# Encoder layer on one core: z multiplied in as the heads' outputs leave PSUM, two buffers in turn for the short convolutions, and operand splits one step ahead

## Chip, cores and metric

The kernel runs on one core of one Trainium2 chip. The metric is the device time of one execution in microseconds (us); lower is better. Times before were taken in three runs, and one more execution was recorded by the hardware profiler.

## The reference, cut to what matters

One layer of a bidirectional encoder over 16 learned tokens and 1024 tokens, with a width of 1024, in float32:

```
h = RMSNorm(x); proj = h @ w_in
q, k, v, z, beta, a, sc_b, sc_c, sc_x, gate_a, gate_b = split(proj)
# branch A, 8 heads of 128: gated delta rule over chunks of 64, forward and backward
o   = o_fwd + o_bwd
o   = o * rsqrt(mean(o * o) + eps) * norm_w
o   = o * silu(z)
y_a = o @ w_branch_dn
# branch B: centred short convolution of width 3
y_b = (sc_b * dwconv3(sc_c * sc_x)) @ w_branch_sc
merged = sigmoid(gate_a) * y_a + sigmoid(gate_b) * y_b
x = x + merged @ w_out
x = x + SwiGLU(RMSNorm(x));  out = RMSNorm(x)
```

## The kernel before

Matmul operands in float32 are split in two parts, high and low, and a product is made of three matmuls (high by high, high by low, low by high). The engines' operations go through a small recorder, so the trace puts nearly all of them down to its line 189; the text goes by names of tiles instead.

**Phase 1 (0 to about 912 us)** has its order written out while the program is built. A model of the engines (class `Clock`) holds a time for each engine, and `run_streams` (line 1186) lets one of several generators go on whenever the modelled TensorE time has reached the time that it asked for. TensorE's filler is the projection `h @ w_in`, 128 columns at a time (`dense_steps`, tile `pm`). Between its matmuls run the steps of the eight heads: `g_decay`, `g_norm`, `g_meta`, `g_inv` (the inverse of a triangular matrix of 64 by 64, with tiles `W`, `XT`, `NP` and `T`), `g_vals`, `g_scan` (the recurrence, with state `S`) and `g_out`. VectorE has lanes of jobs of its own: convolutions of q, k and v, short convolutions, and a substitution.

What comes out of a projection is one of these. `u_z` (line 642) puts silu(z) of a head, in two halves of 128x512, through the buffer `rb` into the DRAM tensor `z_d`. `u_short` with `i` 0 or 1 builds the product of two projections, and then `short_job` (line 588) makes its convolution: for each half one scaling on ScalarE and two multiply-adds on VectorE, in the buffer `yb`, and a store to `yc_d`. `u_short` with `i` = 2 loads both halves again, into `rb` and `yb`, multiplies them with the third projection and stores them to `p_d`. `rb` (`half_buffer`, line 528) and `yb` (`conv_buffer`, line 531) are one buffer each.

`g_out` (line 1074) normalises a head's output, scales four chunks at a time by ScalarE, turns them by TensorE into a PSUM bank `pv`, takes that out by ScalarE with the norm's weight as the scale (`o<-pv,cols`) and stores it to `o_d`.

**The block products (about 915 to 1229 us).** Four stages, called `gb`, `ga` (the two gates), `sc` and `dn` (the two branches), each make a product of 1024x1024 by 1024x1024 out of seven products A to G of half the size (`seven`, line 1592). A product has four steps of 12 matmuls. Each step needs one quarter of its operand split, by ScalarE (`raw` or `wh`, high) and VectorE (`raw` or `wl`, low), into a ring of buffers (`halved`, line 1580). `between` lists work that is written in between the steps: loads of the next stage's blocks, their sums and differences (`by_two`, tiles `pair`), and in `gb` and `ga` also `times_z` (line 1692), which loads a head's `o_d` and `z_d`, multiplies them on VectorE (tiles `w` and `t`) and stores `o_d` again. `evict` takes finished banks out (tiles `s`). A scheduler with a model of its own puts these instructions in order on each engine.

After that come the projection by `w_out`, SwiGLU and the last norm, to the end of the span.

The lines in question of `short_job`, `seven` and `g_out` are among these:

Of the kernel before, what the change touches and what calls it, by code (L numbers as in the profile page):

```python
# [202 lines left out]
def encoder_layer(ctx: ExitStack, tc: tile.TileContext, x, meta, norm1_w, w_in,  # L203
# [323 lines left out]

    def half_buffer():
        return d1.tile([P, 512], F32, tag="rb", name=uid("rb"), bufs=1)

    def conv_buffer():
        return d1.tile([P, 512], F32, tag="yb", name=uid("yb"), bufs=1)

# [53 lines left out]

    def short_job(cx, j, ycs):
        for i in range(2):
            yc = conv_buffer()  # L590
            ycs.append(yc)
            nc.scalar.activation(yc[:, :512], cx[:, 1 + 512 * i:513 + 512 * i], AF.Copy, scale=cols[:, j:j + 1])
            yield A()
            for t in range(1, 3):
                nc.vector.scalar_tensor_tensor(out=yc[:, :512], in0=cx[:, 1 + t + 512 * i:1 + t + 512 * i + 512],
                                               scalar=cols[:, 8 * t + j:8 * t + j + 1], in1=yc[:, :512],
                                               op0=ALU.mult, op1=ALU.add)
                V()
                yield T["dve"] + DEP
            nc.sync.dma_start(yc_d[j][:, 512 * i:512 * i + 512], yc[:, :512])  # L600

    def u_short(j, i, w):
        st_ = shorts[j]
        if i < 2:
# [15 lines left out]
            if i == 1:  # L620
                run_late(True)
                st_["yc"] = []
                st_["job"] = enqueue("short", short_job(st_["cx"], j, st_["yc"]))
                raws[st_["ri"]] = st_["job"]
            else:
                st_["ri"] = len(raws) - 1
        else:
            force(shorts[-1]["job"])
            run_late(True)
            ycs = [half_buffer(), conv_buffer()]  # L630
            for i2 in range(2):
                nc.sync.dma_start(ycs[i2], yc_d[j][:, 512 * i2:512 * i2 + 512])
            for i2 in range(2):
                po = psm()
                yield from dense_steps(po, w, hx, META + 512 * i2, 512)

                def evict(yc=ycs[i2], po=po, i2=i2):
                    nc.vector.tensor_tensor(out=yc, in0=po, in1=yc, op=ALU.mult)
                    nc.sync.dma_start(p_d[j][:, 512 * i2:512 * i2 + 512], yc)
                later(pe(), evict)  # L640

    def u_z(h, w):

        for i in range(2):
# [3 lines left out]
            def evict(po=po, i=i):  # L648
                th = half_buffer()[:, :512]
                nc.scalar.activation(th, po, AF.Silu)  # L650
                nc.sync.dma_start(z_d[h][:, 512 * i:512 * i + 512], th)
            later(pe(), evict)

# [420 lines left out]
    def g_out(h, st_):  # L1074
# [14 lines left out]
        while not job.done:  # L1089
            yield T["pe"] + 300  # L1090
        yield after(y)
        for c4 in range(2):
            oT = O[:, 4 * c4:4 * c4 + 4]
            for c in range(4):
                nc.scalar.activation(oacc[4 * c4 + c], oacc[4 * c4 + c], AF.Copy, scale=y[:, 4 * c4 + c:4 * c4 + c + 1])
# [5 lines left out]
            for c in range(4):  # L1101
                transpose(pt[:, c], oacc[4 * c4 + c])
            yield pe()
            nc.scalar.activation(oT, pt, AF.Copy, scale=cols[:, 24:25])
            t = A()
            lock["scan"] = None
# [484 lines left out]

    def seven(pairs, X, Y, tok, evict, between, moving={}, snap=snap, last_first=False):

        p1s = u2s = p5s = None
        ready = []
        for n, (key, bank, first) in enumerate((("A", X, True), ("B", Y, True), ("C", X, False), ("D", Y, True),
# [3 lines left out]
            for k in range(4):  # L1600
                h_, l_ = ready.pop(0) if ready else halved(pairs[key], k, 512 if key in moving else D)
                bh, bl = moving[key](k) if key in moving else (h_[:, hi], l_[:, hi])
                for t in range(4):
                    c = slice(t * P, t * P + P)
                    for j, (a, b) in enumerate(((h_, bh), (h_, bl), (l_, bh))):
                        fresh = first and k == j == 0
                        mm(bank[t], a[:, c], b, start=fresh, stop=first and k == 3 and j == 2,
                           skip_group_check=not first)
                for f in between[n][1 + k]:
                    f()  # L1610
# [12 lines left out]
            else:  # L1623
                if last_first and n == 5:
                    ready = [halved(pairs["G"], k, D) for k in range(4)]
                evict(*((0, tok[0], bank, p1s), (1, tok[1], bank, p5s), (0, tok[1], bank, u2s))[(1, 4, 5).index(n)])
# [64 lines left out]

    def times_z(j):
        o_ = big("w2", [P, D], F32)
        nc.sync.dma_start(o_, o_d[j])
        for h_ in halves:
            z_ = tp.tile([P, 512], F32, tag="t2", name=uid("t2"), bufs=2)
            nc.sync.dma_start(z_, z_d[j][:, h_])
            nc.vector.tensor_tensor(out=o_[:, h_], in0=o_[:, h_], in1=z_, op=ALU.mult)
        nc.sync.dma_start(o_d[j], o_)

    during_gb = [
# [25 lines left out]
    for d, X, Y, dst, during in ((gb, bank_m, bank_d, tb_d, during_gb), (ga, bank_d, bank_m, ta_d, during_ga)):  # L1727
        seven(d, X, Y, (0, 1), evict_gate(dst), during, {"A": states(0, 0), "B": states(1, 0), "F": states(1, 1)},
              lambda n: pieces())

# [38 lines left out]
    def o_block(key, kh, half):  # L1769
# [17 lines left out]
        [[lambda: new(dn_, "D", "ah0")], [], [], [], []]]  # L1787
    seven(sc, bank_m, bank_d, (0, 1), evict_sc, during_sc)

# [388 lines left out]
```

## Time and profile before

| what | value |
|---|---|
| runs | 1958.40, 1960.96, 1962.62 us |
| median | 1960.96 us |
| profiled execution | 1964.22 us, its span 1962.50 us |
| granted clock of TensorE in it, mean | 0.998 |
| DMA, whole span | 275.76 MB, 141 GB/s |

A page of the profile gives the busy time of each engine and its share of the span; PE is TensorE, DVE VectorE, ACT ScalarE, POOL GpSimd and SP SyncE, which issues the DMAs. In a row of a timeline stand start and duration in us, engine, line, operation, `out<-in` by names of tiles, the shape, and in brackets how long the engine was idle before it and what released it. A row of waits says who waited for whom: us in total, how often, and the longest. A row of windows has the stretch, its length, and for PE, its weight loads, DVE, ACT and POOL the busy time with the number of instructions, then the granted clock of TensorE, the DMA share and GB/s. A row of a tile has the shortest, median and longest duration in ns and the first and last start. A row of DMA issues has their number, the KB of each and the median us from issue to landing.

The slices of the page show which part of the span has idle engines and busy DMA queues (40 slices of 49 us; phase 1 ends in the 19th, the block products in the 25th):

```profile
PE   8999999999999999999999999999999999999998
DVE  4767578887877867744667798559887887756564
ACT  5685587767777675432554545234232332324343
DMA  4132221212121111456797633332666645587654
```

### The profile page before, as it was taken

The page shows a single profiled execution, that of the slowest core. Times are in us where ns is not written, and L with a number is a line of the kernel's source. Part 1 is how long each engine was busy: PE and PEld are TensorE (multiplying, and loading weights), DVE is VectorE, ACT ScalarE, POOL GpSimd, SP SyncE. Part 2 cuts the span into 40 slices and gives each one's busy share as a digit, 9 for nine tenths or more (in the row PEclk, how much of TensorE's full clock was granted, in tenths as well). Part 3 has the DMA queues.
Part 4 walks back from the last instruction along what each step waited for, and adds up shares of the span by engine and source line. Part 5 has one row for each costly group of instructions (what it writes and reads, how often), then busy time and mean ns, then how long its engine had stood idle before and what let it go on. Part 6 is the DMA issues. An engine that isn't in the chain of part 4 may idle for free.

```text
span 1962.5 us, 32157 instructions
## 1 busy us (share of the span) xinstructions
PE 1932.2 (98%) x11914; PEld 1696.9 (86%) x11914; DVE 1415.7 (72%) x2733; ACT 987.8 (50%) x2202; POOL 157.2 (8%) x497
## 2 busy tenths in 40 slices
PE   8999999999999999999999999999999999999998
PEld 8998899999999999988877888887888888888887
DVE  4767578887877867744667798559887887756564
ACT  5685587767777675432554545234232332324343
POOL 2132201120202020000000000000000000000001
PEclk9999999999999999999999999999999999999999
DMA  4132221212121111456797633332666645587654
GB/s 145 46 92 83 68 61 44 71 45 58 53 63 53 49 55 50 146 160 239 282 320 280 212 99 118 107 129 70 212 224 219 208 159 168 176 283 239 195 174 162
DMA packets 221682, 275.76 MB, mean 141 GB/s; under 512 B 15140, under 2 KB 134341, under 8 KB 220117
## 3 DMA queue, kind: packets, MB, share of 16 engines
q1 hardware_dynamic: 221525, 273.72, 42.8%
q8 instruction: 93, 1.52, 0.3%
q14 instruction: 64, 0.52, 0.1%
HBM read 197.03 MB, written 76.63 MB: 139 GB/s over the span
## 4 chain that ended last, share of the span: by engine, by line
PE 80%; DVE 8%; ACT 6%; DMA 3%; issue 1%; POOL 0%; SPq 0%; POOLq 0%; DVEq 0%; ACTq 0%
PE pm L189 42%; PE pd L189 17%; PE pe L189 14%; PE pv L189 7%; DVE kq L189 1%; DMA yc_d<-yb 1%; ACT L189 1%; ACT NP L189 1%; DVE wl L189 1%; DMA o_d<-w 1%; DMA w<-o_d 1%; DVE pair L189 1%; DVE al L189 1%; DVE s L189 1%; ACT kq L189 1%
## 5 line engine op out<-in xcount | busy, mean ns | idle before, releaser
L189 PE MATMUL pm<-hTh,wh 128*128 128x384 f32 (+4 forms) x1234 | 441.9, 359 | 0.1
L189 PE MATMUL pm<-al,wh 128*128 128x384 f32 (+4 forms) x1234 | 413.7, 336 | 0.5 <-DVE al L189 0.5
L189 PE MATMUL pm<-hTh,wl 128*128 128x384 f32 (+4 forms) x1234 | 413.0, 336 | 0.0
L189 PEld LDWEIGHTS pm<-hTh,wh 128*128 128x128 f32 x1234 | 233.0, 189 | 11.4
L189 PEld LDWEIGHTS pm<-al,wh 128*128 128x128 f32 x1234 | 233.2, 189 | 10.6 <-DVE al L189 0.7
L189 PEld LDWEIGHTS pm<-hTh,wl 128*128 128x128 f32 x1234 | 231.8, 188 | 11.3
L189 DVE TENSOR_TENSOR wl<-raw,wh 128x512 fp32r<-128x512 f32 (+1 forms) x132 | 103.3, 783 | 43.3 <-ACT wh L189 43.0
L189 DVE TENSOR_TENSOR al<-raw,ring_h 128x1024 fp32r<-128x1024 f32 x73 | 88.4, 1223 | 63.7 <-ACT ring_h L189 63.3
L189 ACT CAST ring_h<-raw 128x1024 fp32r<-128x1024 f32 x73 | 77.1, 1056 | 109.9 <-PE pv L189 35.3
L189 ACT CAST wh<-raw 128x512 fp32r<-128x512 f32 (+1 forms) x134 | 93.8, 706 | 57.1 <-PE pm L189 20.2
L189 ACT CAST raw<-pair 128x1024 fp32r<-128x1024 f32 (+1 forms) x56 | 53.9, 963 | 94.0 <-PE pe L189 31.4
L189 DVE SCALAR_TENSOR_TENSOR kq<-ra,wc,kq 128x520 f32<-128x520 f32 (+1 forms) x128 | 96.0, 751 | 7.2 <-ACT kq L189 5.2
L189 POOL TENSOR_SCALAR ss<-ss 128x1 f32<-128x1 f32 x13 | 4.6, 351 | 1056.8 <-ACT b L189 602.8
L189 ACT CAST wh<-pair 128x1024 fp32r<-128x1024 f32 (+1 forms) x56 | 53.8, 962 | 59.7 <-PE pv L189 29.7
L189 DVE TENSOR_TENSOR raw<-pair,raw 128x1024 fp32r<-128x1024 f32 (+1 forms) x56 | 62.1, 1109 | 29.2 <-ACT raw L189 29.1
L189 ACT ACTIVATE w<-pd,small 128x128 f32<-128x128 f32 x128 | 40.3, 367 | 81.1 <-PE pd L189 68.0
L189 DVE TENSOR_TENSOR wl<-pair,wh 128x1024 fp32r<-128x1024 f32 (+1 forms) x56 | 62.1, 1109 | 24.1 <-ACT wh L189 24.0
L189 PE MATMUL pd<-S,kq 128*128 128x128 f32 x480 | 74.9, 276 | 1.3 <-DVE S L189 1.3
L189 PEld LDWEIGHTS pd<-S,kq 128*128 128x128 f32 x480 | 66.5, 191 | 3.1 <-DVE S L189 2.1
L189 DVE TENSOR_TENSOR fP<-fP,tm 128x126 f32<-128x126 f32 (+22 forms) x248 | 62.9, 254 | 6.4
L189 DVE TENSOR_TENSOR tm<-fP,fN 128x126 f32<-128x126 f32 (+22 forms) x248 | 62.9, 254 | 6.2
L189 POOL TENSOR_TENSOR small<-small,minus_half 128x9 f32<-128x9 f32 x16 | 30.2, 1886 | 396.0 <-DVE small L189 396.0
(493 smaller groups left out, 4739.8 us busy)
## 6 DMA issues: line engine op xcount, KB each, us to landing
raw<-in_w_in_dram SPq DMA_DIRECT2D x56, 512.0 KB, 4.0
raw<-in_w_gate_up_dram SPq DMA_DIRECT2D x44, 512.0 KB, 5.0
sums<-in_w_down_dram SPq DMA_DIRECT2D x22, 512.0 KB, 5.0
t_d<-sums SPq DMA_DIRECT2D x11, 1024.0 KB, 3.9
raw<-s_d SPq DMA_DIRECT2D x44, 256.0 KB, 3.5
raw<-t_d SPq DMA_DIRECT2D x44, 256.0 KB, 4.0
act_d<-b SPq DMA_DIRECT2D x43, 256.0 KB, 2.7
pair<-in_w_in_dram SPq DMA_DIRECT2D x10, 1024.0 KB, 10.3
```

Of the source, the lines that this page charges most:

```text
L189: r = f(*a, **kw)
```

## The change

It has three parts.

1. **z.** `times_z` is removed from `gb` and `ga`. In `g_out` each half of a head loads its half of `z_d` before the four scalings, and the PSUM bank is taken out by one VectorE operation, (bank x norm weight) x z, in place of ScalarE's.
2. **Buffers.** `rb` and `yb` become `rb0` and `rb1`, which are handed out in turn. A set of held buffers keeps one from being handed out while a job still uses it: the z half of `g_out`, each half of `short_job`, and each half that `u_short` loads, whose two loads now go out one by one. Where none is free, the generator waits in the model's time.
3. **Splits.** In `seven`, `split_next` writes the split for the next step right after a step's matmuls, ahead of the work in `between` and of the evictions. With `then`, the last step of a stage writes the first split of the next stage.

The diff, cut to its core:

```diff
-    def half_buffer():
-        return d1.tile([P, 512], F32, tag="rb", name=uid("rb"), bufs=1)
-    def conv_buffer():
-        return d1.tile([P, 512], F32, tag="yb", name=uid("yb"), bufs=1)
+    held_halves = set()
+    next_half = [0]
+    def free_halves():
+        return [i for i in (next_half[0], 1 - next_half[0]) if i not in held_halves]
+    def half_buffer(hold=False):
+        if not free_halves():
+            force(shorts[-1]["job"])
+        i = free_halves()[0]
+        next_half[0] = 1 - i
+        t = d1.tile([P, 512], F32, tag=f"rb{i}", name=uid("rb"), bufs=1)
+        if hold:
+            held_halves.add(i)
+            return t, i
+        return t
...
-    def short_job(cx, j, ycs):
+    def short_job(cx, j):
         for i in range(2):
-            yc = conv_buffer()
-            ycs.append(yc)
+            while not free_halves():
+                yield T["pe"] + 200
+            yc, held = half_buffer(True)
+            yield max(clock.known(yc, True), after(cx))
             nc.scalar.activation(yc[:, :512], cx[:, 1 + 512 * i:513 + 512 * i], AF.Copy, scale=cols[:, j:j + 1])
...
             nc.sync.dma_start(yc_d[j][:, 512 * i:512 * i + 512], yc[:, :512])
+            held_halves.discard(held)
...
     def g_out(h, st_):
...
+            yield clock.known(z_, True)
+            nc.sync.dma_start(z_, z_d[h][:, c4 * 512:(c4 + 1) * 512])
             for c in range(4):
                 nc.scalar.activation(oacc[4 * c4 + c], oacc[4 * c4 + c], AF.Copy, scale=y[:, 4 * c4 + c:4 * c4 + c + 1])
...
-            yield pe()
-            nc.scalar.activation(oT, pt, AF.Copy, scale=cols[:, 24:25])
-            t = A()
+            yield max(pe(), after(z_))
+            nc.vector.scalar_tensor_tensor(out=oT, in0=pt, scalar=cols[:, 24:25], in1=z_.rearrange("p (c t) -> p c t", c=4),
+                                           op0=ALU.mult, op1=ALU.mult)
+            t = V()
+            held_halves.discard(held)
...
+        def split_next(n, k):
+            n, k = n + (k == 3), (k + 1) % 4
+            if n == 7:
+                if then:
+                    ready.append(halved(then[0]["A"], 0, then[1]))
+                return
+            key = "ABCDEFG"[n]
+            if not ready:
+                ready.extend(halved(pairs[key], q, 512 if key in moving else D)
+                             for q in (range(4) if last_first and n == 6 else (k,)))
...
+                split_next(n, k)
                 for f in between[n][1 + k]:
                     f()
...
-    def times_z(j):
-        o_ = big("w2", [P, D], F32)
-        nc.sync.dma_start(o_, o_d[j])
-        for h_ in halves:
-            z_ = tp.tile([P, 512], F32, tag="t2", name=uid("t2"), bufs=2)
-            nc.sync.dma_start(z_, z_d[j][:, h_])
-            nc.vector.tensor_tensor(out=o_[:, h_], in0=o_[:, h_], in1=z_, op=ALU.mult)
-        nc.sync.dma_start(o_d[j], o_)
...
-    for j in range(H):
-        during_gb[1 + j // 2][2 + 2 * (j % 2)].append(lambda j=j: times_z(j))
```

Both programs have the same matmuls in number and form. VectorE keeps its number of operations (16 `w<-w,t` go, 16 `o<-pv,cols,rb` come), ScalarE has 16 fewer, and SP issues 32 DMAs less (8 `w<-o_d`, 16 `t<-z_d` and 8 `o_d<-w` of 12.6 MB in all) and 16 more (`rb<-z_d`, 4.2 MB).

**What moves: a head's inverse, ScalarE.** The first rows are of before, in the inverse of a head at about 619 us. `yb_8348` is the second half of a short convolution, whose first half went to `yc_d` shortly before; `NP` and `T` belong to the inverse, `ra` and `vT` to a projection and its convolution.

```order
L189 COPY ra_8229<-pm_8232 128x320
L189 ACTIVATE vT_7261<-pm_8232,wc 128x320
L189 ACTIVATE yb_8348<-ra_7661,cols 128x512
L189 COPY NP_693<-W_8287 32x8x32 x2
L189 COPY NP_693<-XT_8254 32x8x32 x2
L189 ACTIVATE T_1352_8353<-pv_8354 128x256
```

After the change the same place on ScalarE reads as follows; the convolution's half is now in one of the two `rb` buffers.

```order
L189 ACTIVATE v_1348_8267<-pd_8184,small_5147 128x128
L189 COPY NP_693<-W_8281 32x8x32 x2
L189 COPY NP_693<-XT_8254 32x8x32 x2
L189 ACTIVATE T_1354_8304<-pv_8305 128x256
L189 ACTIVATE rb_8357<-ra_7649,cols 128x512
L189 ACTIVATE jk_8365,small_5147<-o_7446 128x128
```

The convolution's second half stood ahead of `NP` and `T` and now stands behind them.

**What moves: gb, products F and G, VectorE.** Before, around 980 to 987 us: `raw` and `wl` of `pair_11749` are the splits of the four steps of product G, `w<-w,t` is `times_z`, and the four `s` take out the banks of product F.

```order
L189 TENSOR_TENSOR wl_12373<-pair_11749,wh_12372 128x1024
L189 TENSOR_TENSOR pair_12274<-pair_12175,pair_11898 128x2x512 x2
L189 TENSOR_TENSOR w_1957_12069<-w_1957_12069,t_1958_12071 128x512
L189 TENSOR_TENSOR w_1957_12069<-w_1957_12069,t_1959_12074 128x512
L189 TENSOR_TENSOR s_1960_12078<-pe_11824,s_1960_12078 128x512
L189 TENSOR_TENSOR s_1960_12078<-pd_11825,s_1960_12078 128x512
L189 TENSOR_TENSOR s_1961_12079<-pd_11826,s_1961_12079 128x512
L189 TENSOR_TENSOR s_1961_12079<-pv_11827,s_1961_12079 128x512
L189 TENSOR_TENSOR raw_2009_12391<-pair_11749,raw_2008_12390 128x1024
```

After, at the same place on VectorE (`pair_11781` is the operand of product G here):

```order
L189 TENSOR_TENSOR wl_12333<-pair_11781,wh_12332 128x1024
L189 TENSOR_TENSOR s_1966_12078<-pe_11856,s_1966_12078 128x512
L189 TENSOR_TENSOR raw_2001_12349<-pair_11781,raw_2000_12348 128x1024
L189 TENSOR_TENSOR s_1966_12078<-pd_11857,s_1966_12078 128x512
L189 TENSOR_TENSOR s_1967_12079<-pd_11858,s_1967_12079 128x512
L189 TENSOR_TENSOR s_1967_12079<-pv_11859,s_1967_12079 128x512
L189 TENSOR_TENSOR wl_12367<-pair_11781,wh_12366 128x1024
```

The split of the third step (`raw`) stood behind two sums, `times_z` and four evictions; now it stands behind one eviction.

**What moves: ga, products F and G, VectorE.** Before, around 1051 to 1062 us: the `pair` sums prepare the blocks of the next stage, `raw_2070` and `wl_12875` are the splits of the last two steps of product F, and `raw_2075` is the first of product G.

```order
L189 TENSOR_TENSOR s_2054_12730<-pv_11827,s_2054_12730 128x512
L189 TENSOR_TENSOR pair_12819<-pair_12659,pair_12505 128x2x512 x2
L189 TENSOR_TENSOR pair_12659<-pair_12735,pair_12659 128x2x512 x2
L189 TENSOR_TENSOR raw_2070_12857<-pair_12354,raw_2069_12856 128x512
L189 TENSOR_TENSOR pair_12735<-pair_12735,pair_12659 128x2x512 x2
L189 TENSOR_TENSOR wl_12875<-pair_12354,wh_12874 128x512
L189 TENSOR_TENSOR raw_2075_12909<-pair_12432,raw_2074_12908 128x1024
```

After, the same place on VectorE:

```order
L189 TENSOR_TENSOR s_2048_12694<-pv_11859,s_2048_12694 128x512
L189 TENSOR_TENSOR pair_12783<-pair_12623,pair_12469 128x2x512 x2
L189 TENSOR_TENSOR raw_2062_12815<-pair_12318,raw_2061_12814 128x512
L189 TENSOR_TENSOR pair_12623<-pair_12699,pair_12623 128x2x512 x2
L189 TENSOR_TENSOR wl_12833<-pair_12318,wh_12832 128x512
L189 TENSOR_TENSOR pair_12699<-pair_12699,pair_12623 128x2x512 x2
L189 TENSOR_TENSOR raw_2066_12851<-pair_12396,raw_2065_12850 128x1024
```

One `pair` sum fewer stands ahead of the first split, and the second split has moved ahead of the third sum; the sums themselves are the same.

More of the change, by code (lines that the diff above doesn't have):

```diff
@@ L621, in u_short @@
                 run_late(True)
-                st_["yc"] = []
-                st_["job"] = enqueue("short", short_job(st_["cx"], j, st_["yc"]))
+                st_["job"] = enqueue("short", short_job(st_["cx"], j))
                 raws[st_["ri"]] = st_["job"]
@@ L629, in u_short, with evict @@
             run_late(True)
-            ycs = [half_buffer(), conv_buffer()]
             for i2 in range(2):
-                nc.sync.dma_start(ycs[i2], yc_d[j][:, 512 * i2:512 * i2 + 512])
-            for i2 in range(2):
+                while not free_halves():
+                    T["pe"] += 100
+                    yield
+                yc, held = half_buffer(True)
+                nc.sync.dma_start(yc, yc_d[j][:, 512 * i2:512 * i2 + 512])
                 po = psm()
                 yield from dense_steps(po, w, hx, META + 512 * i2, 512)
-                def evict(yc=ycs[i2], po=po, i2=i2):
+                def evict(yc=yc, held=held, po=po, i2=i2):
                     nc.vector.tensor_tensor(out=yc, in0=po, in1=yc, op=ALU.mult)
                     nc.sync.dma_start(p_d[j][:, 512 * i2:512 * i2 + 512], yc)
+                    held_halves.discard(held)
                 later(pe(), evict)
@@ L651, in evict @@
                 nc.sync.dma_start(z_d[h][:, 512 * i:512 * i + 512], th)
+                heads[h]["z"] = i
             later(pe(), evict)
@@ L1091, in g_out @@
         yield after(y)
+        while not heads[h].get("z"):
+            yield T["pe"] + 300
         for c4 in range(2):
             oT = O[:, 4 * c4:4 * c4 + 4]
+            while not free_halves():
+                yield T["pe"] + 200
+            z_, held = half_buffer(True)
+            yield clock.known(z_, True)
+            nc.sync.dma_start(z_, z_d[h][:, c4 * 512:(c4 + 1) * 512])
             for c in range(4):
@@ L1102, in g_out @@
                 transpose(pt[:, c], oacc[4 * c4 + c])
-            yield pe()
-            nc.scalar.activation(oT, pt, AF.Copy, scale=cols[:, 24:25])
-            t = A()
+            yield max(pe(), after(z_))
+            nc.vector.scalar_tensor_tensor(out=oT, in0=pt, scalar=cols[:, 24:25], in1=z_.rearrange("p (c t) -> p c t", c=4),
+                                           op0=ALU.mult, op1=ALU.mult)
+            t = V()
+            held_halves.discard(held)
             lock["scan"] = None
@@ L1590, in snap, with seven @@
         return [keep_[:, t] for t in range(4)]
-    def seven(pairs, X, Y, tok, evict, between, moving={}, snap=snap, last_first=False):
+    ready = []
+    def seven(pairs, X, Y, tok, evict, between, moving={}, snap=snap, last_first=False, then=None):
         p1s = u2s = p5s = None
-        ready = []
+        def split_next(n, k):
[8 more added lines that the diff above has]
+                             for q in (range(4) if last_first and n == 6 else (k,)))
         for n, (key, bank, first) in enumerate((("A", X, True), ("B", Y, True), ("C", X, False), ("D", Y, True),
@@ L1623, in seven @@
             else:
-                if last_first and n == 5:
-                    ready = [halved(pairs["G"], k, D) for k in range(4)]
                 evict(*((0, tok[0], bank, p1s), (1, tok[1], bank, p5s), (0, tok[1], bank, u2s))[(1, 4, 5).index(n)])
@@ L1724, in encoder_layer @@
          [lambda: by_two(add, L_(sc, "D"), L_(sc, "C"), L_(sc, "A"))], [], []]]
-    for j in range(H):
-        during_gb[1 + j // 2][2 + 2 * (j % 2)].append(lambda j=j: times_z(j))
-    for d, X, Y, dst, during in ((gb, bank_m, bank_d, tb_d, during_gb), (ga, bank_d, bank_m, ta_d, during_ga)):
+    for d, X, Y, dst, during, then in ((gb, bank_m, bank_d, tb_d, during_gb, (ga, 512)), (ga, bank_d, bank_m, ta_d, during_ga, (sc, D))):
         seven(d, X, Y, (0, 1), evict_gate(dst), during, {"A": states(0, 0), "B": states(1, 0), "F": states(1, 1)},
-              lambda n: pieces())
+              lambda n: pieces(), then=then)
     def sc_late():
@@ L1787, in encoder_layer @@
         [[lambda: new(dn_, "D", "ah0")], [], [], [], []]]
-    seven(sc, bank_m, bank_d, (0, 1), evict_sc, during_sc)
+    seven(sc, bank_m, bank_d, (0, 1), evict_sc, during_sc, then=(dn_, D))
     wo = {}
```

## Prediction

> **What bounds the kernel now.** I read the page first, then the waits of TensorE, then the timeline around each of them, then windows that cut the four stages of block products at the starts of their first matmuls.
>
> ```profile
> PE 1932.2 (98%) x11914; PEld 1696.9 (86%) x11914; DVE 1415.7 (72%) x2733; ACT 987.8 (50%) x2202; POOL 157.2 (8%) x497
> 280.00:912.00 632.00, 623.95 (x5293) 596.41 (x5294) 466.10 (x1299) 398.61 (x1198) 79.34 (x276) 1.00 0.25 73
> PE pv L189 <- ACT T L189: 5.1, 3, 2.6
> PE pm L189 <- DVE raw L189: 4.5, 2, 2.8
> ACT yb L189 <- DMA yc_d<-yb: 17.6, 7, 5.1
> ```
>
> TensorE works 98% of a span of 1962.5 us, so the kernel is bound by its matmuls. The change keeps all of them, in number and form. It can win only what TensorE now stands idle or runs at a lower clock, some 30 us in all, and only at the places that it touches. The second row is the part of phase 1 that is re-ordered: TensorE is idle there for 632.00 - 623.95 = 8.05 us. The two largest waits of TensorE by name are for `T` on ScalarE (the heads' inverses) and for `raw` on VectorE (a split operand). ScalarE itself stands 17.6 us for the store `yc_d<-yb`.
>
> **Phase 1: the short convolution's second half.** `short_job` writes its second half into the one buffer `yb`, so ScalarE's first operation of that half waits until the store of the first half has landed, and everything behind it on ScalarE waits too. The worst place, on SP, ScalarE and TensorE:
>
> ```profile
> 615.11 0.32 SPq L189 DMA_DIRECT2D yc_d<-yb  x1
> 619.47 0.72 ACT L189 ACTIVATE yb<-ra,cols 128x512 f32<-128x512 f32 x1 [3.81 <-DMA yc_d<-yb]
> ...
> 621.89 0.39 ACT L189 ACTIVATE T<-pv 128x256 f32<-128x256 f32 x1
> 622.33 0.26 PE L189 MATMUL pv<-W,T 32*32 32x32 f32 x1 [2.60 <-ACT T L189]
> 712.30 0.21 PE L189 MATMUL pv<-W,T 32*32 32x32 f32 x1 [2.10 <-ACT T L189]
> 532.50 0.21 PE L189 MATMUL pv<-W,T 32*32 32x32 f32 x1 [0.43 <-ACT T L189]
> 820.14 0.73 ACT L189 ACTIVATE yb<-ra,cols 128x512 f32<-128x512 f32 x1 [5.14 <-DMA yc_d<-yb]
> 823.08 0.71 PE L189 MATMUL pd<-S,kq 128*128 128x128 f32 x4 [1.04 <-DVE S L189]
> 622.30:625.80 3.50, 3.47 (x103) 3.23 (x104) 2.40 (x7) 3.50 (x11) 0.00 (x0) 0.51 0.02 5
> 712.30:715.80 3.50, 3.50 (x112) 3.41 (x113) 2.66 (x8) 3.50 (x11) 0.00 (x0) 1.00 0.22 80
> ```
>
> The store goes out at 615.11 and ScalarE is let go at 619.47; 2.4 us later the inverse gets `T`, and TensorE, out of filler, has stood 2.60 us. The same happens at 712.30 and 532.50, and at 823.08 behind the wait at 820.14 (I count that one as caused by it; the row names VectorE, which waits for ScalarE there). Idle in all: 0.43 + 2.60 + 2.10 + 1.04 = 6.2 us, of the 8.05 above. From start to start each is about 0.15 us longer (the column counts from the modelled end of the matmul before), so 6.8. And after 2.60 us of idle the clock in the next 3.5 us is 0.51, where after 2.10 us it is 1.00: 3.5 x 0.49 = 1.7 us more. With two buffers in turn the second half writes the other buffer and none of this waits for the store; in the new order `T` even goes ahead of it. **Removable: 8.5 us.** The cover that must hold is that a buffer is free at these places: the same two buffers now also carry z.
>
> [...]
>
> **Phase 1: z in the heads' outputs.** Sixteen ScalarE operations become VectorE operations, and 16 loads of 256 KB are added.
>
> ```profile
> L189 ACT ACTIVATE o<-pv,cols x16: 672/689/693, 287.0 to 870.1; 128x512 f32<-128x512 f32 x16
> L189 DVE TENSOR_TENSOR rb<-pm,rb x7: 683/692/692, 826.5 to 898.7; 128x512 f32<-128x512 f32 x7
> L189 DVE SCALAR_TENSOR_TENSOR yb<-ra,cols,yb x32: 723/746/754, 357.5 to 821.8; 128x512 f32<-128x512 f32 x32
> yb<-yc_d SPq DMA_DIRECT2D x7, 256.0 KB, 2.6
> rb<-yc_d SPq DMA_DIRECT2D x7, 256.0 KB, 3.7
> t<-z_d SPq DMA_DIRECT2D x16, 256.0 KB, 5.6
> 863.60 1.29 ACT L189 ACTIVATE o<-o,small 128x128 f32<-128x128 f32 x4 [1.10 <-POOL small L189]
> 866.84 0.69 ACT L189 ACTIVATE o<-pv,cols 128x512 f32<-128x512 f32 x1 [1.95 <-PE pv L189]
> ```
>
> The new operation (PSUM, a scalar and an SBUF tile, 128x512) is in no row. Its neighbours are 692 ns (PSUM times SBUF) and 746 ns (the same form from SBUF); I take 0.72, so VectorE gets 16 x 0.72 = 11.5 us and ScalarE loses 16 x 0.689 = 11.0. VectorE is 466.10/632.00 = 74% busy here, so most of that lies in its idle time. The z load goes out before the four scalings of a half; by the last two rows 866.84 - 863.60 = 3.2 us pass until the output is turned out. A load of 256 KB lands in 2.6 to 3.7 us in this phase and in 5.6 in the crowded gates, so VectorE waits from nothing to 2.4 us a half, with what is queued behind it: splits `wl`, convolutions, the scan's `S`. What TensorE pays per us of such a wait can be read from the case above: 17.6 us of ScalarE's waiting cost TensorE 6.8, 39%. At 3.7 us of landing: 16 x 0.5 x 0.39 = 3.1 us; at 2.6 nothing. The other end: ScalarE's 11 us less may remove the 8.05 - 6.2 = 1.9 us of other idle. So **-1.9 to 16 x 1.0 x 0.39 = 6.2 us; I take 1.9**, near the 2.6 and 3.7 of this phase rather than the 5.6, with a little for the new order of the filler.
>
> [...]
>
> **The block products.** A step (12 matmuls) takes 2.72 us: the third window holds 20 steps in 54.4 us without a gap, and the last 56 steps in 152.4.
>
> ```profile
> 914.80:980.20 65.40, 65.40 (x289) 53.97 (x288) 47.23 (x52) 31.57 (x44) 0.00 (x0) 1.00 0.86 309
> 980.20:993.20 13.00, 11.28 (x50) 8.96 (x49) 9.14 (x13) 6.78 (x11) 0.00 (x0) 1.00 0.90 302
> 993.20:1047.60 54.40, 54.40 (x242) 45.04 (x241) 28.63 (x33) 26.53 (x38) 0.00 (x0) 1.00 0.96 333
> 1047.60:1076.40 28.80, 24.72 (x97) 18.75 (x96) 27.01 (x29) 13.04 (x18) 0.00 (x0) 0.94 0.72 249
> 1076.40:1228.80 152.40, 152.40 (x674) 125.95 (x672) 131.17 (x146) 78.51 (x90) 0.00 (x0) 1.00 0.44 144
> ```
>
> So removing `times_z` (16 VectorE multiplications, 12.6 MB of transfers at a DMA share near 0.9) buys nothing in the first, third and fifth window, which have no idle time. There are two losses: 13.0 - 4 x 2.72 = 2.1 us in gb's product G and 28.8 - 8 x 2.72 = 7.0 us in ga's F and G.
>
> ```profile
> 982.91 1.29 DVE L189 TENSOR_TENSOR w<-w,t 128x512 f32<-128x512 f32 x2 [1.42 <-issue]
> ...
> 986.51 1.22 DVE L189 TENSOR_TENSOR raw<-pair,raw 128x1024 fp32r<-128x1024 f32 x1
> 987.78 0.74 PE L189 MATMUL pm<-raw,raw 128*128 128x512 f32 x2 [1.72 <-DVE raw L189]
> 1039.71 0.38 SPq L189 DMA_DIRECT2D pair<-in_w_branch_sc_dram  x1
> 1048.45 2.36 DVE L189 TENSOR_TENSOR pair<-pair,pair 128x1024 f32<-128x1024 f32 x2 [4.78 <-DMA pair<-in_w_branch_sc_dram]
> ...
> 1057.66 0.69 DVE L189 TENSOR_TENSOR raw<-pair,raw 128x512 fp32r<-128x512 f32 x1
> ...
> 1072.50 1.22 DVE L189 TENSOR_TENSOR wl<-pair,wh 128x1024 fp32r<-128x1024 f32 x1
> pair<-in_w_branch_sc_dram SPq DMA_DIRECT2D x5, 1024.0 KB, 7.2
> ```
>
> In gb the split of G's third step stands behind two multiplications of `times_z` (1.29 us, which themselves began 1.42 late) and four evictions. All six are gone from ahead of it in the new order but one eviction. **2.1 us go, whole.**
>
> In ga it is VectorE that is late. Its first sum needs the block of short-conv weights issued at 1039.71, which lands 8.7 us later; from then on VectorE works to 1073.72 (the split of G's last step) almost without a pause: 25.3 us, with 0.9 in it spent waiting for TensorE. Without loss TensorE would want that split at about 1047.6 + 7 x 2.72 + 0.4 = 1067.0. The new order puts the `raw` of 1057.66 behind four half sums rather than six, which moves TensorE's first wait but not the end of this chain; all the same sums are in it. Only an earlier landing helps. The load's issue waits for a buffer that TensorE's own steps free, so it stays near 1039.7; but the queue ahead of it has lost 12.6 MB since 928, and SP's blocked stretch at 1032 to 1039 should lie earlier. The same load has a median of 7.2 us over five; a 512 KB load takes 4.0 on the page in phase 1, and 512 KB more at the 333 GB/s of this window 1.6. Between 5.6 and 8.7 I take 6.2: landing at 1045.9, chain end 1045.9 + 24.4 = 1070.3, some 3.2 us late. **Gain 7.0 - 3.2 = 3.8 us (0 to 6.5).** The lower clock of 0.94 lies inside this chain and is not counted again. The four `pair<-p_d` behind it land no later than now.
>
> `then` splits the next stage's first operand early; the stage borders show no idle, so it is worth nothing. The tail behind 1228.8 is unchanged.
>
> **Sum.** -8.5 + 1.9 - 2.1 - 3.8 = -12.5 us on the profiled execution's 1964.22 (span 1962.50): 1951.7. That execution is 3.26 us above the median of the runs shown, 1960.96, so **1948.5 us** on their scale.
>
> **The rivals.**
> - ga's stall stays: the landing is set by the buffer, not by the queue, and VectorE's chain starts at 1048.45 as now. For it speaks that DMA share is only 0.72 in that window; against it, that SP spends 6.36 us on eight issues just before. The gain is 8.7: 1952.3.
> - The heads' outputs give back the gain of phase 1: the two buffers are both held (one by z until its multiplication is done, one by a store in flight), the second half of a convolution waits again and TensorE with it, or a new wait above 2.5 us halves the clock once or twice. Then phase 1 is worth 0 to 2 instead of 6.6: some 1954.
> - All goes: ga's landing is early enough or its sums find room before it, and the z loads are hidden: 8.5 + 2.1 + 6.5 = 17.1: 1943.9.
> - **Slower**: VectorE runs in order, and each z multiplication waits for its own load behind SP's other issues. Loads that land in 5.6 us, as in the gates, less 3.2 of cover are 2.4 us a half; 16 x 2.4 x 0.39 = 15 us, plus 1.7 for each stall above 2.5 us. The gain before this term is 14.4 us, so it decides from 0.9 us of TensorE a half. With three half-clock stretches: 1946.6 + 15 + 5.1 = 1966.7. Against it: the DMA share here is 0.25.
>
> This kernel's measurement tells about 0.2% (3.9 us), so faster means below 1957.0 and slower above 1964.9.
>
> **Chances.** Forecast 0.48, all goes 0.14, ga stays 0.15, heads' outputs give it back 0.14, slower 0.05, and 0.04 for an order of the filler that is worse in ways not named, near no change. The range takes in the first four and the end of the unknown costs (6.2 instead of 1.9 gives 1952.8, with ga's stall kept as well 1956.6; -1.9 where all else goes gives 1942.0): 1942 to 1957. Faster: 0.87. Within 0.2%: 0.08. Slower: 0.05.
>
> **What would show it.** Right: no wait of ScalarE for `yc_d` stores; TensorE's waits for `T` gone, and clock 1.00 around the inverses; the windows of gb's G at 10.9 us and ga's F and G near 25; the weight load at about 1030 (all is earlier by then) landing some 6 us after its issue. Wrong: VectorE waiting for `z_d` loads by more than 10 us in all, new waits of TensorE for `S`, `o` or `wl` in phase 1, ga's window at 28 us still, or a change in the tail.

## The result and the profile after

The changed kernel takes 1947.31 us (median; 1946.62 to 1948.45) against 1961.79 (1958.40 to 1963.29) for the kernel before in the same comparison: a ratio of 0.9929 with a 95% interval of 0.9912 to 0.9946, so 14.5 us less. Forecast were 1948.5 us, in a range of 1942 to 1957. The profiled execution has a span of 1945.7 us, 16.8 us below the one profiled before, which lay some 2 to 3 us above its median. One execution of all those below, of the kernel mul2_order, took 2392.4 us at a mean granted clock of 0.75; medians and ratios leave it out.

The first lines of the page, the waits of TensorE, the tile `rb` and the windows, in this order; the windows are those of the prediction, moved by as much as the stages start earlier (columns as there).

```profile
PE 1928.4 (99%) x11914; PEld 1696.8 (87%) x11914; DVE 1414.7 (73%) x2733; ACT 975.8 (50%) x2186; POOL 162.4 (8%) x497
PE pv L189 <- ACT T L189: 0.7, 1, 0.7
PE pm L189 <- DVE raw L189: 0.8, 1, 0.8
L189 DVE SCALAR_TENSOR_TENSOR o<-pv,cols,rb x16: 728/746/758, 287.5 to 852.4; 128x512 f32<-128x512 f32 x16
280.00:905.00 625.00, 623.90 (x5304) 597.33 (x5303) 475.74 (x1317) 388.93 (x1185) 84.16 (x276) 1.00 0.28 82
970.60:981.50 10.90, 10.90 (x49) 9.02 (x49) 5.03 (x8) 6.14 (x10) 0.00 (x0) 1.00 0.84 287
1035.90:1058.50 22.60, 22.32 (x97) 17.80 (x96) 22.60 (x26) 12.48 (x17) 0.00 (x0) 1.00 0.67 230
```

TensorE's wait for `T` has shrunk from 5.1 to 0.7 us, that for `raw` from 4.5 to 0.8. Phase 1 now loses 625.00 - 623.90 = 1.1 us where it lost 8.05. gb's product G takes 10.9 us, four steps of 2.72, and ga's products F and G 22.6 us where they took 28.8. In ScalarE's list of waits, `yc_d` does not appear any more.

Read from the starts of the matmuls, gb begins at 905.2 us (914.8 before): 9.6 us were won in phase 1. From there to the start of sc the stretch takes 153.3 us (161.6 before): 8.3 us. Then 1.1 us are lost at one step of sc, which before lost nothing, and the tail behind the block products is the same 733.7 us in both. 9.6 + 8.3 - 1.1 = 16.8.

### The profile page after: what moved, and what is told of

Its sections match the earlier page's. It is cut to its first block, busy times and chain, and to the rows that moved or that the text cites. A ratio compares the mean times of both kernels' runs of the same rounds, so it can differ in the third digit from the quotient of the medians.

```text
span 1945.7 us, 32107 instructions
## 1 busy us (share of the span) xinstructions
PE 1928.4 (99%) x11914; PEld 1696.8 (87%) x11914; DVE 1414.7 (73%) x2733; ACT 975.8 (50%) x2186; POOL 162.4 (8%) x497
## 4 chain that ended last, share of the span: by engine, by line
PE 87%; DVE 5%; ACT 4%; DMA 1%; issue 1%; POOL 1%; SPq 0%; POOLq 0%; DVEq 0%; ACTq 0%
PE pm L189 46%; PE pd L189 19%; PE pe L189 14%; PE pv L189 8%; ACT L189 1%; DVE al L189 1%; DVE kq L189 1%; DVE wl L189 1%; ACT PQ L189 0%; ACT NP L189 0%; DVE s L189 0%; DVE NP L189 0%; DVE mA L189 0%; SPq L189 0%; ACT wh L189 0%
## 5 line engine op out<-in xcount | busy, mean ns | idle before, releaser
L189 PEld LDWEIGHTS pm<-hTh,wh 128*128 128x128 f32 x1234 | 232.3, 189 | 11.4 <-ACT hTh L189 0.2
L189 PEld LDWEIGHTS pm<-hTh,wl 128*128 128x128 f32 x1234 | 231.5, 188 | 11.2
```

The lines of the kernel that those rows point to most:

```text
L189: r = f(*a, **kw)
```

## The experiments

Eleven kernels and a repeat of the changed one were run, in three groups, each compared with the kernel before on the same chip, whose median was 1961.6 us beside the first group and 1962.2 beside the other two. The ratios are formed over the runs and not from the two medians, so their fourth place can differ from the quotient of the medians. The table has, of each one's profiled execution, the start of gb, what gb's G loses, how long after its issue the weight block that ga's F waits for lets VectorE go on, and what ga's F and G lose (beyond 2.72 us a step). All are read from the starts of instructions in the trace; in s_only the trace names a `p_d` load as the one that came last there.

| kernel | median us | ratio, interval | gb starts | gb G loses | block lands after | ga F, G lose |
|---|---|---|---|---|---|---|
| before | 1961.6 to 1962.2 | | 914.8 | 2.1 | 8.7 | 7.1 |
| b_only: the buffers | 1953.85 | 0.9963 (0.9950 to 0.9976) | 906.2 | 1.2 | 9.0 | 9.2 |
| s_only: the splits | 1960.33 | 0.9991 (0.9981 to 1.0000) | 912.2 | 1.2 | 7.8 | 3.5 |
| z_only: z in the outputs | 1952.75 | 0.9952 (0.9937 to 0.9967) | 910.1 | 0 | 5.1 | 2.4 |
| zb: z and buffers | 1948.25 | 0.9930 (0.9914 to 0.9947) | 905.4 | 0 | 5.2 | 2.5 |
| bs: buffers and splits | 1954.31 | 0.9955 (0.9940 to 0.9970) | 906.0 | 1.7 | 8.8 | 7.5 |
| after_again: all three | 1947.74 | 0.9931 (0.9909 to 0.9953) | 905.6 | 0 | 5.2 | 0.9 |
| tz_nomul | 1958.16 | 0.9974 (0.9964 to 0.9984) | 914.2 | 0 | 5.1 | 2.4 |
| tz_none | 1955.58 | 0.9962 (0.9948 to 0.9976) | 916.0 | 0 | 5.2 | 2.5 |
| tz_pool | 1977.29 | 1.0080 (1.0053 to 1.0107) | 914.0 | 0 | 5.2 | 2.5 |
| mul2 | 1959.10 | 0.9980 (0.9970 to 0.9990) | 915.0 | 0 | 5.3 | 1.0 |
| mul2_free | 1954.33 | 0.9960 (0.9949 to 0.9971) | 913.5 | 0 | 5.1 | 0.9 |
| mul2_order | 1952.91 | 0.9957 (0.9945 to 0.9970) | 910.3 | 0 | 5.6 | 1.3 |

Five of these (before, s_only, tz_nomul, tz_none, tz_pool) share phase 1 as it was. Their gb starts between 912.2 and 916.0, mean 914.2. Most of that spread goes with the clock: in phase 1, behind its first 20 us, TensorE's clock was at half once in before, tz_nomul and tz_pool (914.0 to 914.8), not at all in s_only (912.2) and twice in tz_none (916.0), for 3.4 us each time, which is 1.7 us of work.

### Each part by itself

b_only puts the rotation into the kernel before and leaves `g_out`, `times_z` and `seven` as they were:

```diff
-    def half_buffer():
-    def conv_buffer():
+    def half_buffer(hold=False):
...
-    def short_job(cx, j, ycs):
+    def short_job(cx, j):
```

> Before, with the two buffers in turn alone (z still multiplied in gb and ga, splits written as before). Theory: TensorE's stalls of phase 1 behind the store yc_d go, 8 to 9.5 us, and nothing else changes: ratio about 0.9955, ScalarE's 17.6 us of waiting for yc_d below 2 us, the first matmul of gb about 9 us earlier than at 914.8, and the block products keep their losses of 2.1 us (gb G) and 7.0 us (ga F and G). Rival: phase 1 was won because ScalarE lost 11 us of work to VectorE, and the buffers matter little: ratio 0.998 or more, with stalls of TensorE for T left.

gb starts 8.1 us before that mean of 914.2, and in ScalarE's waits `yc_d` is gone. The rival of ScalarE's lighter load falls, since ScalarE does all its work here. Of phase 1 and of ga's window in b_only:

```profile
280.00:906.00 626.00, 624.45 (x5305) 597.39 (x5305) 465.46 (x1302) 399.57 (x1201) 80.62 (x276) 1.00 0.25 76
1038.10:1069.10 31.00, 25.83 (x98) 19.55 (x96) 27.01 (x29) 13.10 (x18) 0.00 (x0) 0.89 0.70 243
```

Phase 1 loses 1.6 us; ga's F and G take 31.0 us, 2.2 more than before, so there part of the gain is given back. That happens with the code of ga unchanged: in this execution the landing of the weight block let VectorE go on 2.1 us after the start of F, where it was 0.9 us in before, and the clock was at half for 6.8 us where it was 3.4.

s_only copies the new `seven` and its calls and nothing else:

```diff
-    def seven(pairs, X, Y, tok, evict, between, moving={}, snap=snap, last_first=False):
+    def seven(pairs, X, Y, tok, evict, between, moving={}, snap=snap, last_first=False, then=None):
...
+                split_next(n, k)
```

> Before, with the early splits alone. Theory: what freed the split in gb's G and the chain in ga was that times_z went with its transfers; with times_z in place the splits move little: 0 to 1 us, ratio 0.9995 to 1.0, losses of 2.1 and 7.0 us still there. Rival: the early splits themselves took the block products' 7 to 9 us: ratio about 0.996, both losses gone.

The median is 1.3 us lower and the interval ends at 1.0000; the rival's 0.996 lies outside it. The one profiled execution lost 3.5 us in ga, between the 7.0 of the theory and the nothing of the rival; bs below says why. As `times_z` kept its place ahead of gb's split, a loss of 1.2 us in G is still there.

z_only moves z into `g_out`, with the single `rb` held for it, and removes `times_z`:

```diff
-            nc.scalar.activation(oT, pt, AF.Copy, scale=cols[:, 24:25])
+            nc.vector.scalar_tensor_tensor(out=oT, in0=pt, scalar=cols[:, 24:25], in1=z_.rearrange("p (c t) -> p c t", c=4),
+                                           op0=ALU.mult, op1=ALU.mult)
...
-        during_gb[1 + j // 2][2 + 2 * (j % 2)].append(lambda j=j: times_z(j))
```

> Before, with z in the heads' outputs alone; z is loaded into the one buffer rb, and yb keeps its role. Theory: the block products gain 7 to 8.5 us, phase 1 keeps its stalls behind yc_d and the 16 VectorE multiplications cost 0 to 2 us: ratio 0.9960 to 0.997. Rival: the multiplications and their loads cost phase 1 as much as the block products win, and only the second buffer hides that: ratio 0.999 or more, with VectorE waiting over 10 us for z_d.

It wins 8.9 us in the median, a little more than expected. The block products behave as expected (gb's G loses nothing, ga 2.4 us). The surprise is phase 1: gb starts 4.1 us before the mean of 914.2, though ScalarE still stands 12.8 us for `yc_d` here. None of TensorE's stalls is for `T` any more (2.4 us are for `NP` and `XT` of the inverse), and its clock is never at half in phase 1. Against s_only, which has no half clock there either, it is 2.1 us, and against tz_none below, which has the same losses in the block products, the medians differ by 2.8 us. Which part of the new order does it was not tested.

zb is the changed kernel with the old `seven`:

```diff
-                split_next(n, k)
                 for f in between[n][1 + k]:
                     f()
...
-              lambda n: pieces(), then=then)
+              lambda n: pieces())
```

> The changed kernel without the early splits (z in the heads' outputs and the two buffers only). Theory: it has nearly the whole gain, 14 to 16 us in the profiled spans, ratio about 0.993; gb's G at 10.9 us and the weight block of ga landing some 5 us after its issue. Rival: without early splits the block products lose their 7 to 9 us again: ratio about 0.9955.

The first theory holds: 0.9930, with the changed kernel at 0.9929 and 0.9931. The times do not tell the splits from nothing. The traces do: ga loses 2.5 us here, 0.8 and 0.9 us in the two profiled executions of the changed kernel, at the same landing.

bs has the two buffers and the splits, with `times_z` in place; its edit is that of b_only and s_only together.

> Before, with the two buffers and the early splits, z still multiplied in gb and ga. Theory: the gains add: phase 1 as with the buffers alone (gb starts near 906), ga's loss about 3.5 us as with the splits alone because its first stall stays short of half clock, the weight block still 8 us after its issue: ratio 0.994 to 0.995. Rival: the splits' gain in ga was a chance of the landing in that one execution: ga loses 7 us or more, ratio 0.9960.

The rival is right here, with ga at 7.5 us. The 3.5 us of s_only were mostly an early landing: there the block was in VectorE's hands at the start of F, here 2.3 us after it. The clock adds to it: it was at half for 6.8 us here and not at all in that window of s_only.

### What made ga's weight block late

tz_nomul keeps every transfer of `times_z` and leaves its multiplications out, so z is not applied; tz_none (the second of these edits) leaves out `times_z` whole, again without z:

```diff
-            nc.vector.tensor_tensor(out=o_[:, h_], in0=o_[:, h_], in1=z_, op=ALU.mult)
```

```diff
-    for j in range(H):
-        during_gb[1 + j // 2][2 + 2 * (j % 2)].append(lambda j=j: times_z(j))
```

> Before, with the 16 multiplications of times_z left out and all its transfers kept (z is not applied). Theory: the late weight block of ga comes from the transfers in the queue: it still lands 8 to 9 us after its issue and ga loses 6 to 9 us, while gb's G loses 1 us less; ratio 0.9985 to 1.0. Rival: VectorE's multiplications were what made ga late: landing below 6 us or a loss below 3 us, ratio 0.9965.

> Before, with times_z left out whole, transfers too (z is not applied). Theory: the block lands 5 us after its issue, gb's G loses nothing and ga's F and G about 2.4 us, as with z in the heads' outputs; phase 1 as before: 6 to 7 us less, ratio 0.9965; what the run with z alone has beyond this is a gain in phase 1. Rival: the landing depends on SP's order, not on the bytes: above 7 us still, ratio 0.999.

My theory of tz_nomul falls and the signs of its rival appear: with all 12.6 MB still moved, the block lands 5.1 us after its issue, as it does with none in tz_none, whose theory holds. What differs is SP's order in time. From the timelines of SP and, in the last row of each, of VectorE, of b_only first and of tz_nomul below it (SPq is SP issuing a DMA):

```profile
1021.96 0.32 SPq L189 DMA_DIRECT2D o_d<-w  x1
...
1023.62 0.64 SPq L189 DMA_DIRECT2D pair<-in_w_branch_sc_dram  x1
1024.31 6.43 SPq L189 DMA_DIRECT2D pair<-p_d  x8
1031.16 0.38 SPq L189 DMA_DIRECT2D pair<-in_w_branch_sc_dram  x1
...
1040.16 2.36 DVE L189 TENSOR_TENSOR pair<-pair,pair 128x1024 f32<-128x1024 f32 x2 [5.95 <-DMA pair<-in_w_branch_sc_dram]
```

```profile
1020.88 0.38 SPq L189 DMA_DIRECT2D pair<-in_w_branch_sc_dram  x1
1021.67 6.83 SPq L189 DMA_DIRECT2D pair<-p_d  x8
...
1038.52 0.38 SPq L189 DMA_DIRECT2D pair<-in_w_branch_sc_dram  x1
...
1043.61 2.36 DVE L189 TENSOR_TENSOR pair<-pair,pair 128x1024 f32<-128x1024 f32 x2 [1.12 <-DMA pair<-in_w_branch_sc_dram]
```

In b_only, as in the kernel before, SP comes to a store of `o_d` that has to wait for VectorE's multiplication. Behind it on SP stand a 1 MB weight block and eight loads of 256 KB, and they go out just ahead of the block that ga waits for: 7.5 us lie between the two blocks, and the second lands 9.0 us after its issue. In tz_nomul 17.6 us lie between them, and it is 5.1 us.

tz_pool is the check of this: every byte and every multiplication stays, and only the stores change the queue.

```diff
-        nc.sync.dma_start(o_d[j], o_)
+        nc.gpsimd.dma_start(o_d[j], o_)
```

> Before, with the stores o_d of times_z issued by GpSimd in place of SP; every byte and every multiplication stays. Theory (SP's order): the weight block of ga came late because SP stood before the last such store, and then issued the block ahead of it with its eight p_d loads just before; without the store in SP's row the block lands 5 to 6 us after its issue and ga loses 2 to 3 us instead of 7: ratio 0.9970 to 0.998. Rival (bytes): with all transfers in the queue it lands after 8 us or more as before and ga loses 6 us or more: ratio 0.9995 to 1.0.

For this place the theory holds: landing 5.2 us after the issue, loss in F and G 2.5 us, with 16.6 us between the two blocks. From its timelines of SP and VectorE:

```profile
1041.76 0.38 SPq L189 DMA_DIRECT2D pair<-in_w_branch_sc_dram  x1
...
1058.32 0.38 SPq L189 DMA_DIRECT2D pair<-in_w_branch_sc_dram  x1
...
1063.47 2.36 DVE L189 TENSOR_TENSOR pair<-pair,pair 128x1024 f32<-128x1024 f32 x2 [1.18 <-DMA pair<-in_w_branch_sc_dram]
```

As a kernel it is slower than before, by 15 us: stores from GpSimd land after 6.4 us in the median instead of 4.8, SP issues the next head's load of `w` only behind them (at 1009.30 after the store of 1002.02), and VectorE waits for these loads in front of splits: 33.6 us in all (11.2 before), for instance in this row of its timeline.

```profile
1013.76 1.29 DVE L189 TENSOR_TENSOR w<-w,t 128x512 f32<-128x512 f32 x2 [9.62 <-DMA w<-o_d]
```

So the total expected of tz_pool was missed, while the question it was made for is answered: not the bytes but the order in SP's row delayed the block. The waits stretch ga's products A to E to 71.9 us here (54.4 before), which also spreads the bytes; in tz_nomul they take 55.9, and the block lands as early. That the block ahead of it is what held it up is argued from the spacing; it was not moved alone.

### What a multiplication on VectorE costs in phase 1

mul2 makes each of the 16 multiplications twice:

```diff
+            V()
+            nc.vector.scalar_tensor_tensor(out=oT, in0=pt, scalar=cols[:, 24:25], in1=z_.rearrange("p (c t) -> p c t", c=4),
+                                           op0=ALU.mult, op1=ALU.mult)
             t = V()
```

> The changed kernel with each multiplication of a head's output by z made twice, so 16 more VectorE operations of 0.746 us (11.9 us in all); the second writes the same product again. Theory: VectorE has the room and the cost is 0 to 1 us against the changed kernel (ratio 0.9925 to 0.9935 against before). Rival: TensorE pays 39% of it, 4.7 us (ratio 0.995).

Both theories are far off: it costs 11.4 us against the changed kernel as measured beside the next group. Since phase 1 is ordered by a model that counts the added operations, the whole order had changed with them. Two more kernels take that apart, beside a repeat of the changed kernel.

> The changed kernel once more, on the same chip as the three beside it, as their measure: ratio 0.992 to 0.9935 against before.

mul2_free issues the second multiplication past the model, so nothing else moves; mul2_order (the second edit) tells the model of it and issues nothing:

```diff
+            tc.nc.vector.scalar_tensor_tensor(out=oT, in0=pt, scalar=cols[:, 24:25], in1=z_.rearrange("p (c t) -> p c t", c=4),
+                                           op0=ALU.mult, op1=ALU.mult)
```

```diff
+            clock.did("dve", "scalar_tensor_tensor", (), dict(out=oT, in0=pt, scalar=cols[:, 24:25], in1=z_.rearrange("p (c t) -> p c t", c=4),
+                                           op0=ALU.mult, op1=ALU.mult))
```

> The changed kernel with the second multiplication issued past the model of the engines, so that the order on TensorE, ScalarE and SP is that of the changed kernel, row for row, and VectorE alone has 16 operations of 0.746 us more (the same product is written again). Theory: it was the order that cost 11 us in the run before, not the work; here the cost is 0 to 2 us. Rival: VectorE's 11.9 us themselves delay TensorE by 39% or more: 4.7 to 11 us.

> The changed kernel with its own work (16 multiplications), but the model of the engines is told of 16 more, so that phase 1 has the order of the run with doubled multiplications, up to some 40 rows. Theory (order): nearly as slow as that run, 7 to 11 us above the changed kernel, with the gap of 3.7 us ahead of gb. Rival (work): within 2 us of the changed kernel.

after_again measures 1947.74 us, mul2_free 1954.33 (+6.6) and mul2_order 1952.91 (+5.2): work alone and order alone each cost about half of what both cost together in mul2 (+11.4). In mul2_free the theory falls and the rival about the work is right, 6.6 us for 11.9 us of VectorE; in mul2_order both theory (7 to 11 us) and rival (within 2) miss. The next rows are of mul2_free, TensorE's waits and a piece of its timeline; L1130 is the added operation.

```profile
PE pv L189 <- DVE o L1130: 2.7, 5, 0.9
531.57 0.63 PE L189 MATMUL pv<-ident,o 128*128 128x128 f32 x4 [0.93 <-DVE o L1130]
```

Part of it is not VectorE's time but PSUM: `pv` is one bank, and the second reading keeps it 0.75 us longer from the transposes behind. These waits are 2.7 of the 6.6 us; the other 3.9 are 33% of 11.9, near the 39% of the rival. In mul2_order the last head's output has moved to the end of phase 1, and there the wait that the prediction feared occurs; from the timelines of VectorE, SP, ScalarE and TensorE:

```profile
901.59 0.75 DVE L189 SCALAR_TENSOR_TENSOR o<-pv,cols,rb 128x512 f32<-128x512 f32 x1 [4.05 <-DMA rb<-z_d]
902.37 0.32 SPq L189 DMA_DIRECT2D o_d<-o  x1
904.44 0.94 SPq L189 DMA_DIRECT2D pair<-in_w_in_dram  x2
909.59 0.62 ACT L189 CAST raw<-pair 128x512 fp32r<-128x512 f32 x1 [13.50 <-DMA pair<-in_w_in_dram]
...
910.30 0.77 PE L189 MATMUL pm<-hTh,raw 128*128 128x512 f32 x1 [2.77 <-issue]
```

VectorE waits 4.05 us for a z load. SP stores this output behind it and then issues gb's first weight blocks, at 904.44, where the changed kernel does so at 897.33; ScalarE has the first block 5.2 us after the issue in both. So gb's first matmul comes after a gap of 2.77 us that the changed kernel does not have, and the granted clock of the 3.5 us behind it is 0.50. This execution took 1955.43 us, 2.5 above the median of its kernel.

## Why the prediction was right, step by step

**What bounds it.** Right: all matmuls stayed, TensorE's idle time was what could be won, and the tail and sc's and dn's full steps did not move.

**Phase 1, -8.5 us by the buffers.** Shown: b_only wins 8.6 us there against the profiled execution of before, on which the sum was made, and 8.1 us against the mean of five executions in the old order. The cause is as stated, ScalarE's second half behind the store of the first.

**Phase 1, +1.9 us by z.** Too much: with the buffers, z adds nothing (gb at 905.4 in zb, 906.2 in b_only). The operation is 746 ns where I took 0.72 us. The loads land in 3.2 us, against the 3.2 us of cover that the prediction read, and VectorE waited for one once, as the waits of the changed kernel have it:

```profile
DVE o L189 <- DMA rb<-z_d: 0.6, 1, 0.6
rb<-z_d SPq DMA_DIRECT2D x16, 256.0 KB, 3.2
```

But the reason given, that VectorE's idle 26% hides the work, is not what the runs show. Work that the build does not know of costs 6.6 us for 11.9. That it was hidden because ScalarE was relieved and the order was made anew around it is argued; no run relieves ScalarE alone. z_only shows that such a new order can be worth 2 to 4 us of itself, mul2_order that it can cost 5.

**gb, -2.1 us.** Right in size and cause: the loss is gone in every kernel without the multiplications of `times_z`, and 1.2 us of it stay with the splits alone. Its size differs between executions, though: it is 1.2 us in b_only too, where the code of gb is that of before.

**ga, -3.8 us; measured -6.2.** The direction is right, the term is too small, and two of its steps failed.
- "The queue ahead of it has lost 12.6 MB since 928" is not the cause; tz_nomul and tz_pool keep the bytes and have the early landing. "SP's blocked stretch" in the same sentence is, as tz_pool shows, and the landing was 5.1 us, not 6.2. The changed kernel, SP and VectorE:

```profile
1006.37 0.41 SPq L189 DMA_DIRECT2D pair<-in_w_branch_sc_dram  x1
...
1028.06 0.38 SPq L189 DMA_DIRECT2D pair<-in_w_branch_sc_dram  x1
1033.17 2.36 DVE L189 TENSOR_TENSOR pair<-pair,pair 128x1024 f32<-128x1024 f32 x2 [1.15 <-DMA pair<-in_w_branch_sc_dram]
...
1049.39 1.21 DVE L189 TENSOR_TENSOR wl<-pair,wh 128x1024 fp32r<-128x1024 f32 x1
1050.52 2.35 DVE L189 TENSOR_TENSOR pair<-pair,pair 128x1024 f32<-128x1024 f32 x2
...
1056.20 1.22 DVE L189 TENSOR_TENSOR wl<-pair,wh 128x1024 fp32r<-128x1024 f32 x1
```

- "Only an earlier landing helps" is wrong by some 1.6 us. The chain's end is the same with and without the early splits: the last `wl` ends 21.5 us after the start of F here and 21.6 in zb. But TensorE, whose order mixes the steps of G, waits for splits in the middle of the chain. In zb the `wl` of G's second step stands behind two half sums and TensorE waits for it; in the changed kernel it stands ahead of them, and TensorE's wait in the last of the rows below has no counterpart. From VectorE's and TensorE's timelines of zb:

```profile
1049.68 2.36 DVE L189 TENSOR_TENSOR pair<-pair,pair 128x1024 f32<-128x1024 f32 x2
1051.94 1.22 DVE L189 TENSOR_TENSOR wl<-pair,wh 128x1024 fp32r<-128x1024 f32 x1
...
1053.22 0.50 PE L189 MATMUL pe<-wl,wh 128*128 128x512 f32 x1 [0.57 <-DVE wl L189]
```

**sc, not foreseen, +1.1 us.** One step of sc waits for its split, which VectorE reaches late behind a sum that waited for the next stage's weights. It is 1.1 us in one execution of the changed kernel and 0.3 in the other, so it hangs on a landing; no run was made for it.

**The rivals.** "All goes" (1943.9) is nearest to what the trace shows: z hidden, ga's loss all but gone. The two profiled executions lie 16.8 us apart where the sum had 12.5; phase 1 gave 3.0 us more (9.6 for 6.6), ga 2.4 more, and sc took 1.1. That the median still came out 1.2 us from the forecast is in part luck: the profiled execution of before, against which the sum was made, lay 2.4 us above the median of the comparison, by stalls that differ from run to run. The slower rival's mechanism is real, as mul2_order shows, though in an order that costs some 5 us in all and not where the change has put its loads. Its limit of 2.5 us for a stall that halves the clock was an estimate between two rows (1.00 behind 2.10 us, 0.51 behind 2.60), and it does not hold: the clock was 0.52 behind 1.83 us and 1.00 behind 3.02, as the last section shows.

## What to carry to other kernels

- A wait on an engine's critical chain for a store to land was cured here by a second buffer, at the size read from the trace (8.5 us read, 8.6 measured in b_only): sum the idle time of the bound engine behind it, not that of the waiting engine (8 us of 17.6 here, 1.7 of it by the clock).
- A load that lands late may have been queued badly rather than crowded out (7.8 to 9.0 us from the issue here with such a store ahead of it on SP, 5.1 in tz_nomul with the same bytes): look in the issuing engine's row for a store that waits for another engine and holds back what stands behind it.
- In a program whose order is made by a model, adding an operation changes two things, and they can be measured apart (6.6 us for the work and 5.2 for the order here) by hiding the operation from the model or the model's entry from the program.

## What the hardware showed that was not expected

In these traces the length of a stall did not by itself decide whether TensorE's clock fell. The granted clock in the 3.5 us behind a stall was 0.52 after 1.83 us of idle (tz_none), 0.66 after 2.13 (tz_nomul), 0.51 after 2.60 (before), but 1.00 after 2.10 (before) and after 3.02 (tz_pool). The first two rows are of tz_none, the other two of tz_pool.

```profile
712.25 0.21 PE L189 MATMUL pv<-W,T 32*32 32x32 f32 x1 [1.83 <-ACT T L189]
712.25:715.75 3.50, 3.50 (x104) 3.26 (x105) 2.68 (x8) 3.50 (x11) 0.00 (x0) 0.52 0.22 80
978.25 0.50 PE L189 MATMUL pe<-hTh,raw 128*128 128x512 f32 x1 [3.02 <-DVE raw L189]
978.25:981.75 3.50, 3.50 (x15) 2.93 (x16) 3.50 (x4) 2.96 (x4) 0.00 (x0) 1.00 0.68 257
```

Where the idle time fell went with it. In before, between 5 and 1960 us, the granted clock was at half (0.50) in two stretches of 3.41 us, from 622.32 and from 1059.23: 436.9 us apart, which is 128 times 3.413. In tz_none the starts of two lie 26 times 3.41 us apart (the granted clock was 0.70 in the 3.5 us from 622.27, and 0.50 in the stretch from 712.42). With before cut into stretches of 3.41 us through its two starts, TensorE was idle for 2.59 us in sum in the one ahead of each, and for 1.49 us at most in any other between 8 and 1957 us; the stall of 2.10 us fell on two of them, with 0.87 and 1.23 us of idle time. Cut in the same way, the stall of 1.83 us in tz_none lay inside one stretch, and the next was at half clock; the stall of 3.02 us in tz_pool fell on two, with 1.44 and 1.58 us of idle time. In all of these, half clock came behind 1.83 us or more of idle time in one stretch, and not behind 1.58 us or less. No run moved a stall against the stretches; that its place among them decides is an estimate from these rows. Of before first (four rows), then of tz_none, then of tz_pool (two each):

```profile
618.91:622.32 3.41, 0.82 (x6) 0.54 (x4) 1.69 (x3) 2.74 (x7) 0.00 (x0) 1.00 0.03 9
622.32:625.73 3.41, 3.40 (x103) 3.16 (x104) 2.33 (x7) 3.41 (x11) 0.00 (x0) 0.50 0.02 5
707.66:711.07 3.41, 2.54 (x16) 2.19 (x14) 1.53 (x3) 1.59 (x4) 0.12 (x2) 1.00 0.38 113
711.07:714.48 3.41, 2.18 (x103) 2.09 (x104) 2.89 (x7) 3.35 (x11) 0.00 (x0) 1.00 0.23 82
709.00:712.42 3.42, 1.59 (x37) 1.32 (x40) 2.27 (x4) 2.92 (x7) 0.00 (x0) 1.00 0.04 12
712.42:715.83 3.41, 3.41 (x104) 3.17 (x92) 2.59 (x8) 3.40 (x12) 0.00 (x0) 0.50 0.23 82
973.26:976.67 3.41, 1.97 (x9) 1.31 (x7) 3.41 (x6) 0.83 (x2) 0.53 (x1) 1.00 1.05 399
976.68:980.09 3.41, 1.83 (x8) 1.54 (x9) 3.41 (x6) 3.41 (x5) 0.00 (x0) 1.00 0.95 336
```

The spread between executions goes with the clock. The runs of the kernel before lie between 1956.6 and 1966.6 us over the nineteen beside the last group: the six with a mean granted clock of 0.999 took 1956.6 to 1960.1, the eight with 0.998 took 1960.8 to 1964.4, the four with 0.997 or 0.996 took 1963.4 to 1966.6, and one with 0.969 took 1965.3. The changed kernel, whose two traces have no half clock between the first 10 and the last 5 us, lies between 1946.6 and 1949.0.
